# Block 3's two-direction recurrence: both directions in one set of tiles instead of one after the other

## The chip, the cores and the metric

The kernel runs on one core of a Trainium2 chip. Its engines work side by side, each through its own list of instructions: TensorE (PE; its weight loads are PEld), VectorE (DVE), ScalarE (ACT), GpSimd (POOL) and SyncE (SP), whose queue issues nearly all transfers from HBM. The metric is device time in microseconds (us). TensorE's clock has two levels here, 1.2 and 2.4 GHz, shown as a granted clock of 0.50 and 1.00.

## The reference

Three transformer blocks run one after the other on 256 tokens of width 1024, in fp32. The change is in the third block. Its input projection feeds a neighborhood attention, a memory attention, a recurrence (RWKV-7) in both directions, and three gates; the gated branches are merged, and an expert-choice layer with 16 experts of three weight matrices each follows. Of the recurrence (6 heads of 64 channels) this matters:

```python
for d in range(2):
    def mix(t, mu):
        return t + (token_shift(t, d) - t) * mu
    r = mix(p_r, mu_rkv[d, 0]); k = mix(p_k, mu_rkv[d, 1]); v = mix(p_v, mu_rkv[d, 2])
    w_log = -jax.nn.softplus(-(w0[d] + jnp.tanh(mix(lat_w, mu_w[d])) @ w2[d])) - 0.5
    decay = jnp.exp(-jnp.exp(w_log))
    a = jax.nn.sigmoid(a0[d] + mix(lat_a, mu_a[d]) @ a2[d])
    ...
    y_sum = y_sum + wkv7_scan(rh, to_heads_3(decay, RW_HEADS), kh, vh, -kk, kk * ah, reverse=(d == 1))
    bonus_sum = bonus_sum + jnp.sum(rh * kh * r_k, axis=-1, keepdims=True) * vh
```

`wkv7_scan` updates a 64 x 64 state per head with every token, from the first to the last for d = 0 and from the last to the first for d = 1. The two directions share no state; only their outputs are added, and a group norm over the sum follows.

## The kernel before

Matrix products with large weights are split: a weight tile w comes by DMA, ScalarE rounds it to wh (L303), VectorE takes the rest to wl (L305; four times GpSimd does it in this stage), and TensorE makes three products per tile, xh·wh, xl·wh and xh·wl (L314 to L316, output psg). Those of the third block's gates are called gate products here: 12 chunks of 48, 576 in all, and nothing in the recurrence needs them. A scheduler (Tile) writes each engine's list ahead of time and puts gate products between those of the recurrence and of the attentions.

`rwkv` runs the recurrence in a chunked form, two chunks of 128 tokens. For each direction in turn: the token shift is mixed in (subtractions on GpSimd L1353 and L1359, then VectorE L1354 and L1361); low-rank products plw and pla (L1369, L1370) and ScalarE's tanh give the decay and the gate a; VectorE sums the logarithm of the decay over a chunk with one scan per chunk and per 128 channels (L1387) and centres it (L1392); key norms (pnk), the bonus term (pbo), and the multiplication of keys and queries with the decays (L1438 to L1441) follow; v and bk are transposed on TensorE (pvt, pbt); the score products pka (L1465), masked, make 12 matrices of 128 x 128 (6 heads, 2 chunks), whose triangular inverse is needed.

`tri_inv` forms that inverse for n matrices at once. ScalarE copies the 32 x 32 blocks of the diagonal into one tile, VectorE transposes it (L550), eliminates in 14 steps of a multiplication and an addition (L560, L562), which work on all blocks at once in the other layout, and transposes back twice (L565, L566). TensorE then builds the larger blocks from the small ones (tpx, tpu: L575, L582, L604 to L633).

The scan itself goes chunk by chunk: masked scores pkm and pkr, then prh, psa and py, and pzt, which carries the state to the second chunk. `end` closes the recurrence with the group norm (pgm, pgv, pgg). The second direction begins with its own plw when the first one's last py are done, and its matrices are lower triangular, so tri_inv also has the mirrored form.

After it come the merges of the three branches (weights mg3a and mg3b, products psg on ona, omm and orw), the output product on mgh and mgl, the routing, and the experts. An expert's weights are loaded whole, 1 MB at a time, into slots: rings that exist all along, and the pools of which ES lists the sizes, which take over memory that earlier stages give up (`K.slots()` looks for it). SP issues its list in order; a load whose slot is still in use holds those behind it.

Of the kernel before, what the change touches and what calls it, by code (L numbers as in the profile page):

```python
# [25 lines left out]
def const_arrays():  # L26
# [4 lines left out]
    lo = (i > j).astype(np.float32)  # L31
# [12 lines left out]
    c["mk1"] = np.concatenate([lo, loi], 1)  # L44
# [40 lines left out]
    "b3": ["bd64", "mk1", "u16"],  # L85
    "b3a": ["mk0", "l16"],
# [135 lines left out]
ES = [2, 3, 1, 4, 3]  # L222
# [6 lines left out]
class Core:  # L229
# [308 lines left out]
    def tri_inv(self, first, pool, n, a, upper, want, out, tags):  # L538
        nc = self.nc
        P, W = [128, 1280], [128, max(1056, 96 * n)]  # L540
# [31 lines left out]
        px = self.psum([128, n, 32], "tpx")  # L572
        for i in range(n):
            for q in range(4):
                nc.tensor.matmul(px[qs[q], i], a[qs[q], i, qs[q]], mc[qs[q], i], start=True, stop=True)  # L575
        nc.vector.tensor_tensor(x, px, self.C("l16" if upper else "u16")[:, None, :].to_broadcast([128, n, 32]), op=ALU.mult)
        pu = []
        for lh, rh in ((oc, x), (x, oc)):
            pu.append(self.psum([128, n, 32], "tpu"))
            for i in range(n):  # L580
                for q in range(4):
                    nc.tensor.matmul(pu[-1][qs[q], i], lh[qs[q], i], rh[qs[q], i], start=True, stop=True)  # L582
        for d, p in zip((mc, oc), pu):
            nc.vector.tensor_tensor(d, d, p, op=ALU.add)
# [14 lines left out]
        px = self.psum([128, n, 32], "tpx")  # L599
        pm = self.psum([128, n, 32], "tpu")  # L600
        po = self.psum([128, n, 32], "tpu")
        for i in range(n):
            for r, c in pairs:
                nc.tensor.matmul(px[qs[r], i], a[qs[c], i, qs[r]], mc[qs[c], i], start=True, stop=True)  # L604
        for r, c in pairs:
            nc.scalar.copy(x[qs[r]], px[qs[r]])
        todo = [(r, c, half.start <= 32 * r < half.stop) for r, c in pairs]
        for i in range(n):
            for r, c, here in todo:
                if want == "m" or here:  # L610
                    nc.tensor.matmul(pm[qs[r], i], oc[qs[r], i], x[qs[r], i], start=True, stop=True)
        for i in range(n):
            for r, c, here in todo:
                if want == "o" or here:
                    nc.tensor.matmul(po[qs[c], i], x[qs[r], i], oc[qs[r], i], start=True, stop=True)
        for r, c in pairs:
            here = half.start <= 32 * r < half.stop
            (a0, p0, b0), (a1, p1, b1) = ((c, po, r), (r, pm, c)) if want == "o" else ((r, pm, c), (c, po, r))
            nc.vector.tensor_copy(out[qs[a0], :, qs[b0]], p0[qs[a0]])
            if here:  # L620
                nc.scalar.copy(oth[qs[a1], :, 32 * (b1 % 2):32 * (b1 % 2) + 32], p1[qs[a1]])
        x = w[:, 32 * n:96 * n].rearrange("p (i c) -> p i c", c=64)
# [696 lines left out]
def rwkv(K, keep, pool, tri, early, pp, lat, latg, y_out):  # L1319
# [18 lines left out]
    exps = []  # L1338

    for d in range(2):  # L1340
        sh = slice(0, S) if d == 0 else slice(2, S + 2)
        ar = pool.tile([128, 3, 2, S], F32, tag="ar", name="ar")
        bk = pool.tile([128, 3, 2, S], F32, tag="bk", name="bk")
        vs = pool.tile([128, 2, 3, S], F32, tag="vs", name="vs")
        vv, sq = vs[:, 0], vs[:, 1]
        aa = pool.tile(T3, F32, tag="aa", name="aa")
        km = pool.tile(T3, F32, tag="km", name="km")
        ce = pool.tile([128, 2, 3, 2, 129], F32, tag="om", name="ce")
        cn, ee = ce[:, 0], ce[:, 1]
        lm = early.tile([128, S], F32, tag="lm", name="lm")  # L1350


        nc.gpsimd.tensor_tensor(lm, lat[:, sh], lat[:, cur], op=ALU.subtract)  # L1353
        nc.vector.scalar_tensor_tensor(lm, lm, V("mu_wa", d), lat[:, cur], op0=ALU.mult, op1=ALU.add)  # L1354
        with K.behind(exps[0] if d else None):
            nc.scalar.activation(lm[0:64], lm[0:64], AF.Tanh)
        for n, dst in ((0, ar[:, :, 1]), (1, km), (2, vv)):
            src = pp[:, 3 * n:3 * n + 3]
            nc.gpsimd.tensor_tensor(dst, src[:, :, sh], src[:, :, cur], op=ALU.subtract)  # L1359
            for f in range(3):  # L1360
                nc.vector.scalar_tensor_tensor(dst[:, f], dst[:, f], V("mu_rkv", (d * 3 + n) * 3 + f), src[:, f, cur],  # L1361
                                               op0=ALU.mult, op1=ALU.add)


        for f in range(3):
            pw = K.psum([128, 2, 128], "plw")
            pa = K.psum([128, S], "pla")
            fs = slice(f * 128, f * 128 + 128)
            nc.tensor.matmul(pw, lora[0:64, d, fs], lm[0:64], start=True, stop=True)  # L1369
            nc.tensor.matmul(pa, lora[64:128, d, fs], lm[64:128], start=True, stop=True)  # L1370
            nc.scalar.activation(ee[:, f, :, 0:128], pw, AF.Tanh, scale=0.5,
                                 bias=hw0[:, 3 * d + f:3 * d + f + 1])
            tanh = nc.scalar.activation(aa[:, f], pa, AF.Tanh, scale=0.5, bias=ha0[:, 3 * d + f:3 * d + f + 1])
        hs = 0.5 * math.exp(-0.5)
        for f in range(3):
            e = ee[:, f, :, 0:128]
            nc.vector.tensor_scalar(e, e, hs, hs, op0=ALU.mult, op1=ALU.add)
        nc.vector.tensor_scalar(aa, aa, 0.5, 0.5, op0=ALU.mult, op1=ALU.add)

        o, z = (1, 0) if d == 0 else (0, 128)  # L1380
        for f in range(3):
            for c in range(2):
                src, dst = ee[:, f, c, 0:128], cn[:, f, c, o:o + 128]
                if d == 1:
                    src, dst = src[:, ::-1], dst[:, ::-1]
                nc.gpsimd.memset(cn[:, f, c, z:z + 1], 0.0)
                nc.vector.tensor_tensor_scan(dst, src, src, 0.0, op0=ALU.add, op1=ALU.bypass)  # L1387
        rho = pool.tile([128, 3, 2], F32, tag="rho", name="rho")
        nc.vector.tensor_copy(rho, cn[:, :, :, 64])
        for f in range(3):  # L1390
            for c in range(2):
                nc.vector.tensor_scalar(cn[:, f, c], cn[:, f, c], rho[:, f, c:c + 1], None, op0=ALU.subtract)  # L1392

        c0, c1 = (0, 1) if d == 0 else (1, 0)
        zc = pool.tile([128, 3], F32, tag="zc", name="zc")
        last = 128 if d == 0 else 0
        nc.vector.tensor_tensor(zc, cn[:, :, c0, last], rho[:, :, c1], op=ALU.add)
        nc.scalar.activation(zc, zc, AF.Exp, scale=-1.0)
        fl = lambda t: t.rearrange("p f c t -> p (f c t)")
        nc.scalar.activation(fl(ee), fl(cn), AF.Exp, scale=-1.0)  # L1400
        nc.scalar.activation(fl(cn), fl(cn), AF.Exp)


        kk = ar[:, :, 0]
        for f in range(3):
            nc.vector.tensor_scalar(kk[:, f], km[:, f], V("k_k", f), None, op0=ALU.mult)
        nc.scalar.activation(sq, kk, AF.Square)
        ln = K.ln_set(tanh)
        for f0, f1 in ((0, 2), (2, 3)):
            pn = K.psum([128, f1 - f0, S], "pnk")  # L1410
# [624 lines left out]
```

## Time and profile before

| | |
|---|---|
| median of 3 runs | 1989.26 us (1987.42 to 1989.70) |
| profiled execution | 1989.29 us, its span 1987.5 us |
| busy share of the span | PE 83%, PEld 54%, DVE 40%, ACT 30%, POOL 5% |
| mean granted TensorE clock | 0.918 |
| DMA | 557.20 MB, mean 280 GB/s |
| idle time of PE before expert products, mostly for DMA (L1887, L1959) | 154.6 and 49.4 us |

The first thing to read is the place of a stage on the time line: the first two blocks lie before about 750 us, the recurrence of the third from about 768 to 990, merges and routing to 1049, and the experts after it. The busy shares are means over these, with a different limit in each. A window's length less PE's busy time is PE's idle time in it.

### The profile page before, as it was taken

How to read it: one execution, taken by the hardware profiler on the slowest of the kernel's cores; microseconds unless marked ns; L12 is line 12 of the kernel's file. 1: busy time of each engine (PE TensorE's matmuls, PEld its weight loads, DVE VectorE, ACT ScalarE, POOL GpSimd, SP SyncE). 2: the span in 40 equal slices, each digit the busy share in tenths (PEclk: the TensorE clock that was granted, in tenths of full speed). 3: DMA queues.
4: the chain of work that ended last, by engine and by line, in shares of the span. 5: the costliest groups of instructions: out<-in, count | busy, mean ns of one | idle time of the engine just before them, and what ended most of it. 6: DMA issues, size and time to landing. Idle time of an engine off the chain costs nothing.

```text
span 1987.5 us, 28807 instructions
## 1 busy us (share of the span) xinstructions
PE 1657.6 (83%) x11882; PEld 1064.1 (54%) x11882; DVE 792.3 (40%) x1617; ACT 597.0 (30%) x1180; POOL 101.3 (5%) x140
## 2 busy tenths in 40 slices
PE   3999989999999999998989776777777677767776
PEld 2998989898999999777873111111111111111111
DVE  7798767657655577758472000000000000000001
ACT  3656455655555456534351000000000000000001
POOL 0000010000000110112011000000000000000000
PEclk9999989999999999979899988888878889877888
DMA  8443643345455554205388999999999999999998
GB/s 297 170 149 107 220 159 128 128 154 176 178 175 178 185 198 149 86 22 202 118 326 354 413 414 414 417 416 415 416 416 415 416 416 414 414 415 418 418 416 294
DMA packets 107062, 557.20 MB, mean 280 GB/s; under 512 B 10545, under 2 KB 17201, under 8 KB 62002
## 3 DMA queue, kind: packets, MB, share of 16 engines
q1 hardware_dynamic: 106930, 555.36, 71.9%
q8 instruction: 93, 1.52, 0.3%
q14 instruction: 39, 0.32, 0.0%
HBM read 554.27 MB, written 1.05 MB: 279 GB/s over the span
## 4 chain that ended last, share of the span: by engine, by line
PE 44%; DMA 43%; DVE 8%; ACT 2%; issue 1%; SPq 1%; POOL 0%; DVEq 0%; ACTq 0%; POOLq 0%
DMA w<-in_w_eu 12%; DMA w<-in_w_eg 11%; PE psg L316 10%; PE psg L314 10%; PE psg L315 10%; DMA w<-in_w_ed 7%; DMA wwh<-in_w_eu 4%; DMA wwl<-in_w_eg 4%; DMA wwh<-in_w_ed 3%; DVE wl L305 2%; PE pgu L1887 1%; DVE w L657 1%; PE pd L1959 1%; DMA wwh<-in_w_eg 1%; DMA wwl<-in_w_eu 1%
## 5 line engine op out<-in xcount | busy, mean ns | idle before, releaser
L1887 PE MATMUL pgu<-w,xe 128*32 128x512 f32 x1768 | 306.5, 788 | 154.6 <-DMA w<-in_w_eu 88.9
L305 DVE TENSOR_TENSOR wl<-w,wh 128x512 fp32r<-128x512 f32 (+1 forms) x510 | 330.1, 689 | 173.7 <-ACT wh L303 159.7
L303 ACT CAST wh<-w 128x512 fp32r<-128x512 f32 x516 | 288.1, 607 | 257.8 <-PE psg L315 223.8
L1887 PEld LDWEIGHTS pgu<-w,xe 128*32 128x32 f32 x1768 | 43.1, 122 | 396.6 <-DMA w<-in_w_eu 224.5
L1959 PE MATMUL pd<-w,at 128*32 128x512 f32 x808 | 183.7, 616 | 49.4 <-DMA w<-in_w_ed 44.1
L1937 DVE TENSOR_TENSOR gg<-gg,pgu 128x512 f32<-128x512 f32 x16 | 11.0, 688 | 508.0 <-PE pgu L1887 504.4
L1959 PEld LDWEIGHTS pd<-w,at 128*32 128x32 f32 x808 | 41.2, 112 | 183.0 <-DMA w<-in_w_ed 114.3
L1962 DVE COPY ye<-pd 128x512 f32<-128x512 f32 x15 | 10.4, 692 | 290.4 <-PE pd L1959 290.4
L1942 ACT COPY at<-pat 128x512 f32<-128x512 f32 x16 | 9.4, 585 | 311.5 <-PE pat L1940 311.5
L314 PE MATMUL psg<-h1h,wh 128*128 128x256 f32 x352 | 102.8, 292 | 0.0
L316 PE MATMUL psg<-h1h,wl 128*128 128x256 f32 x352 | 101.9, 290 | 0.0
L315 PE MATMUL psg<-h1l,wh 128*128 128x256 f32 x352 | 101.4, 288 | 0.0
L315 PE MATMUL psg<-n3hl,wh 128*128 128x256 f32 x344 | 100.7, 293 | 0.0
L316 PE MATMUL psg<-n3hh,wl 128*128 128x256 f32 x344 | 100.2, 291 | 0.4 <-DVE wl L305 0.4
L315 PE MATMUL psg<-n2fhl,wh 128*128 128x256 f32 x352 | 100.0, 284 | 0.2
L316 PE MATMUL psg<-n2fhh,wl 128*128 128x256 f32 x352 | 99.7, 283 | 0.0
L314 PE MATMUL psg<-n3hh,wh 128*128 128x256 f32 x344 | 99.6, 290 | 0.0
L314 PE MATMUL psg<-n2fhh,wh 128*128 128x256 f32 x352 | 99.5, 283 | 0.0
L1936 ACT ACTIVATE gg<-pgu 128x512 f32<-128x512 f32 x16 | 9.6, 597 | 277.5 <-PE pgu L1887 277.5
L314 PE MATMUL psg<-n2hh,wh 128*128 128x256 f32 x304 | 87.7, 289 | 2.0 <-ACT n2hh L456 2.0
L315 PE MATMUL psg<-n2hl,wh 128*128 128x256 f32 x304 | 88.4, 291 | 0.1
L316 PE MATMUL psg<-n2hh,wl 128*128 128x256 f32 x304 | 87.8, 289 | 0.0
(729 smaller groups left out, 3430.9 us busy)
## 6 DMA issues: line engine op xcount, KB each, us to landing
w<-in_w_eg SPq DMA_DIRECT2D x112, 1024.0 KB, 18.4
w<-in_w_eu SPq DMA_DIRECT2D x109, 1024.0 KB, 19.9
w<-in_w_ed SPq DMA_DIRECT2D x101, 1024.0 KB, 18.7
w<-in_w_in SPq DMA_DIRECT2D x68, 1024.0 KB, 4.9
w<-in_w_f SPq DMA_DIRECT2D x22, 1024.0 KB, 4.9
w<-in_w_ada SPq DMA_DIRECT2D x12, 1024.0 KB, 6.2
wwh<-in_w_ed SPq DMA_DIRECT2D x19, 512.0 KB, 14.8
wwl<-in_w_ed SPq DMA_DIRECT2D x19, 512.0 KB, 15.0
```

Source lines behind the costliest of these rows:

```text
L303: self.nc.scalar.copy(wh[:, a:b], w[:, k0 + a:k0 + b])
L305: e.tensor_tensor(wl[:, a:b], w[:, k0 + a:k0 + b], wh[:, a:b], op=ALU.subtract)
L314: nc.tensor.matmul(out, a, x[0], start=first, stop=False)
L315: nc.tensor.matmul(out, a, x[1], start=False, stop=False)
L316: nc.tensor.matmul(out, b, x[0], start=False, stop=last)
L657: nc.vector.scalar_tensor_tensor(w[:, f], w[:, f], 1.0, sg, op0=ALU.mult, op1=ALU.mult, accum_out=out[:, j:j + 1])
L1887: nc.tensor.matmul(pg[32 * j:32 * j + 32], xe[:, k, e * 32:e * 32 + 32], w[j // 2][:, j % 2 * 512:j % 2 * 512 + 512], start=k == 0, stop=k ...
L1936: nc.scalar.activation(gg, pgu[0], AF.Silu)
L1937: nc.vector.tensor_tensor(gg, gg, pgu[1], op=ALU.mult)
L1942: last = nc.scalar.copy(at, pt)
L1959: nc.tensor.matmul(pd[hh][32 * q:32 * q + 32], at[:, q, 32 * j:32 * j + 32], w[i][:, hh * 512:hh * 512 + 512], start=j == 0, stop=j == 3)
L1962: nc.vector.tensor_copy(ye[:, 512:1024], pd[1])
```

## The change

Both directions are worked on together. All tiles of the recurrence get a leading or middle index for the direction: 6 groups of 128 channels instead of 3, the second three in reversed time (the sources are read with a step of -1). Then both directions are causal in their own time, the matrices of both are upper triangular, and `tri_inv` is called once with 24 matrices. TensorE's work in it is cut in parts of 12 matrices. The logarithms of a direction's decay are summed by one scan of 774 elements, which a 0 in a tile `one` restarts at each of the six rows. One product of bk with the decay goes to GpSimd. v and bk are transposed behind the inverse instead of ahead of it. In the scan each kind of product is issued for both directions before the next kind. The tiles of the inverse and of the scan's outputs live in pools of their own on the right side of SBUF, those of the merges in a pool opened later, and ES goes from [2, 3, 1, 4, 3] to [3, 3, 5, 2], 13 as before. The number of TensorE's instructions doesn't change (9139); VectorE's falls from 1591 to 1503, ScalarE's from 1138 to 1117, GpSimd's from 145 to 128.

```diff
-ES = [2, 3, 1, 4, 3]
+ES = [3, 3, 5, 2]
...
+        parts = [(i, min(n, i + 12)) for i in range(0, n, 12)]
+        lev = self.C("l16" if upper else "u16")[:, None, :]
+        for i0, i1 in parts:
+            m = i1 - i0
+            px = self.psum([128, m, 32], "tpx")
...
-    for d in range(2):
-        sh = slice(0, S) if d == 0 else slice(2, S + 2)
-        ar = pool.tile([128, 3, 2, S], F32, tag="ar", name="ar")
-        bk = pool.tile([128, 3, 2, S], F32, tag="bk", name="bk")
+    ar = pool.tile([128, 6, 2, S], F32, tag="ar", name="ar")
+    bk = pool.tile([128, 6, 2, S], F32, tag="bk", name="bk")
...
+        for d in range(2):
+            t, c = src[:, :, sh[d]], src[:, :, cur]
+            if d:
+                t, c = t[:, :, ::-1], c[:, :, ::-1]
+            nc.gpsimd.tensor_tensor(dst[:, 3 * d:3 * d + 3], t, c, op=ALU.subtract)
...
-        for f in range(3):
-            for c in range(2):
-                src, dst = ee[:, f, c, 0:128], cn[:, f, c, o:o + 128]
...
-                nc.vector.tensor_tensor_scan(dst, src, src, 0.0, op0=ALU.add, op1=ALU.bypass)
+        nc.vector.tensor_tensor_scan(al(cn[:, ds]), one, al(ee[:, ds]), 0.0, op0=ALU.mult, op1=ALU.add)
...
-        nc.vector.tensor_tensor(ch(bk[:, :, 1]), ch(bk[:, :, 1]), cn[:, :, :, now], op=ALU.mult)
+    nc.gpsimd.tensor_tensor(ch(bk[:, :, 1]), ch(bk[:, :, 1]), cn[:, :, :, now], op=ALU.mult)
...
-        K.tri_inv(pool, tri, 12, ch12(am), d == 0, "o", ch12(om2), ("lr", "t2", "t3", "t4"))
+    with tc.tile_pool(name="tri", bufs=1, side="right") as tri:
+        K.tri_inv(tri, tri, 24, ch24(am), True, "o", ch24(om2), ("t1", "t2", "t3", "t4"))
...
+                ts, y = (cs, py) if d == 0 else (slice((1 - c) * 128, (2 - c) * 128), py[:, :, ::-1])
+                if c == 0:
+                    nc.scalar.copy(ysum[:, :, ts], y)
+                else:
+                    nc.vector.tensor_tensor(ysum[:, :, ts], ysum[:, :, ts], y, op=ALU.add)
...
+    lctx = ExitStack()
+    lp = lctx.enter_context(tc.tile_pool(name="l3", bufs=1))
+    orw = [lp.tile([128, 3, S], F32R, name=f"orw{i}") for i in range(2)]
+    gts[1] = lp.tile([128, 8, S], F32, name="g3b")
```

What this does to the engines' lists shows at three places; x48 stands for 48 instructions in a row (the trace records a product of fp32 operands, which all but psg have here, twice). The first is TensorE where the inverse passes from VectorE back to it, before in the second direction (tri tiles are the inverse's, psg gate products):

```order
L575 MATMUL tpx<-tri_9560,am 32x32 x48
L315 MATMUL psg<-n3hl,wh 128x256
L316 MATMUL psg<-n3hh,wl 128x256
L314 MATMUL psg<-n3hh,wh 128x256
L582 MATMUL tpu<-tri_9564,tri_9561 32x32 x48
L582 MATMUL tpu<-tri_9561,tri_9564 32x32 x48
L604 MATMUL tpx<-tri_9560,am 32x32 x24
```

Between its two halves stand seven gate products. Now, once for both directions (atps, atpt and atpo belong to the attentions):

```order
L576 MATMUL tpx<-tri_8976,am 32x32 x75
L481 MATMUL atps<-nak,naq 128x256 x2
L576 MATMUL tpx<-tri_8976,am 32x32 x21
L585 MATMUL tpu<-tri_8980,tri_8977 32x32 x48
L585 MATMUL tpu<-tri_8977,tri_8980 32x32 x13
L509 MATMUL atpt<-ct_g,atsm 128x128 x2
L585 MATMUL tpu<-tri_8977,tri_8980 32x32
L509 MATMUL atpt<-ct_g,atsm 128x128 x2
L585 MATMUL tpu<-tri_8977,tri_8980 32x32 x34
L585 MATMUL tpu<-tri_8980,tri_8977 32x32 x48
L585 MATMUL tpu<-tri_8977,tri_8980 32x32 x48
L608 MATMUL tpx<-tri_8976,am 32x32 x48
```

The number of tpx is the same over both, 96, and now in one place. Between the last pka and the first of these tpx there were 101 gate products and 32 products of the attentions in the first direction and 143 gate products in the second; now there are 133 and 27.

The second is TensorE in the scan's second chunk, before in the first direction:

```order
L1490 MATMUL pkr<-ar,bk 128x128 x6
L1500 MATMUL prh<-vt,lr 128x64 x3
L1505 MATMUL prh<-zt,ar 128x64 x3
L314 MATMUL psg<-n3hh,wh 128x256
L315 MATMUL psg<-n3hl,wh 128x256
L316 MATMUL psg<-n3hh,wl 128x256
L1500 MATMUL prh<-vt,lr 128x64 x3
L1505 MATMUL prh<-zt,ar 128x64 x3
L1510 MATMUL psa<-rh_9325,om_8919 128x64
L1515 MATMUL py<-lr,vt 64x128 x3
L1510 MATMUL psa<-rh_9325,om_8919 128x64 x5
L1519 MATMUL py<-ar,zt 64x128 x6
```

Four gate products stand between the first and the last prh here. Now:

```order
L1499 MATMUL pkm<-ar,bk 128x256 x12
L1506 MATMUL pkr<-ar,bk 128x128 x12
L1516 MATMUL prh<-vt,lr 128x64 x12
L1521 MATMUL prh<-zt,ar 128x64 x12
L312 MATMUL psg<-n3hl,wh 128x256
L313 MATMUL psg<-n3hh,wl 128x256
L311 MATMUL psg<-n3hh,wh 128x256
L1527 MATMUL psa<-rh_9714,om_8934 128x64 x2
L1527 MATMUL psa<-rh_9714,om_8934 128x64 x10
L1544 MATMUL py<-lr,vt 64x128 x6
L1549 MATMUL py<-ar,zt 64x128 x6
L1553 MATMUL py<-rt_9533,sa_9713 64x128 x6
```

Each kind stands for both directions in one row of products: 24 prh, 36 py. In both scans before there were 18 gate products or other psg, in the joint one 10. Before the last group-norm product pgg there are 171 fewer gate products than before it in the old program; 96 of them follow it in a row.

The third is SP's list from the last input weights (in_w_in) to the merge weights, before:

```order
L287 DMA w<-in_w_in 128x2048
L1870 DMA w<-in_w_eg 128x2048
L287 DMA w<-in_w_in 128x2048
L1870 DMA w<-in_w_eg 128x2048
L287 DMA w<-in_w_in 128x2048
L1870 DMA w<-in_w_eg 128x2048 x2
L287 DMA w<-in_w_mg3a 128x1280
L1870 DMA w<-in_w_eg 128x2048
L287 DMA w<-in_w_mg3a 128x1280 x3
L1870 DMA w<-in_w_eg 128x2048
L287 DMA w<-in_w_mg3b 128x768
```

Expert loads (w_eg) stand between input weights here. Now:

```order
L284 DMA w<-in_w_mg3a 128x1280
L1885 DMA w<-in_w_eg 128x2048 x6
L284 DMA w<-in_w_mg3a 128x1280
L1885 DMA w<-in_w_eg 128x2048 x2
L284 DMA w<-in_w_mg3a 128x1280
L1885 DMA w<-in_w_eu 128x2048
L284 DMA w<-in_w_mg3a 128x1280
L1885 DMA w<-in_w_eu 128x2048
L284 DMA w<-in_w_mg3b 128x768 x2
L1885 DMA w<-in_w_eu 128x2048
L284 DMA w<-in_w_mg3b 128x768 x2
```

All gate weights now go ahead of the expert loads, and six expert loads stand between the first and the second load of mg3a.

## Rows read from the trace of the kernel before

**Rows 1.** the page, slices of 49.7 us: GB/s moved by DMA.

```profile
GB/s 297 170 149 107 220 159 128 128 154 176 178 175 178 185 198 149 86 22 202 118 326 354 413 414 414 417 416 415 416 416 415 416 416 414 414 415 418 418 416 294
```

**Rows 2.** windows: stretch, length, busy us (instructions) of PE, PEld, DVE, ACT, POOL.

```profile
767.94:795.00 27.06, 25.63 (x192) 22.61 (x192) 26.31 (x59) 19.12 (x39) 2.22 (x2) 1.00 0.34 118
795.00:821.70 26.70, 24.30 (x152) 19.34 (x152) 21.42 (x58) 13.52 (x32) 3.89 (x5) 0.94 0.28 93
821.70:854.30 32.60, 31.51 (x576) 23.14 (x578) 20.57 (x53) 16.75 (x43) 6.31 (x7) 1.00 0.18 56
854.30:882.50 28.20, 26.97 (x195) 22.85 (x193) 9.44 (x20) 4.06 (x10) 3.62 (x9) 0.72 0.11 38
882.50:913.60 31.10, 28.76 (x199) 25.41 (x197) 28.67 (x58) 22.10 (x36) 10.84 (x9) 0.92 0.49 193
913.60:937.30 23.70, 17.42 (x148) 17.21 (x148) 21.05 (x42) 10.24 (x19) 3.06 (x4) 0.95 0.40 143
937.30:956.00 18.70, 17.22 (x495) 16.08 (x495) 7.58 (x11) 6.32 (x13) 1.00 (x2) 0.79 0.12 38
956.00:980.20 24.20, 23.47 (x203) 19.46 (x200) 7.93 (x18) 3.70 (x9) 0.00 (x0) 0.86 0.19 61
980.20:990.00 9.80, 9.80 (x66) 9.00 (x65) 7.42 (x15) 4.86 (x9) 0.00 (x0) 1.00 0.80 279
990.00:1012.00 22.00, 18.58 (x137) 16.80 (x135) 21.68 (x48) 14.47 (x27) 0.00 (x0) 1.00 0.70 254
1012.00:1049.40 37.40, 27.83 (x230) 26.29 (x230) 23.43 (x49) 16.49 (x30) 12.43 (x12) 0.89 0.89 349
```

**Rows 3.** timeline of PE: start, length, line, operation; the first expert product.

```profile
1049.44 1.08 PE L1887 MATMUL pgu<-w,xe 128*32 128x512 f32 x4
```

**Rows 4.** waits of PE, 767.94 to 990 us: total, times, longest.

```profile
PE tpx L575 <- DVE tri L565: 6.6, 2, 6.3
```

**Rows 5.** groups of DVE, second inverse: count, busy us, mean ns.

```profile
L305 DVE TENSOR_TENSOR wl<-w,wh 128x512 fp32r<-128x512 f32 x10 | 6.4, 686 | 0.8 <-ACT wh L303 0.8
L562 DVE TENSOR_TENSOR tri<-tri,tri 128x28 f32<-128x28 f32 (+6 forms) x14 | 5.2, 373 | 0.4
```

**Rows 6.** DVE on tile ce: ns minimum, median, maximum; first, last start.

```profile
L1387 DVE TENSOR_TENSOR_SCAN ce<-ce x12: 394/412/427, 770.3 to 889.6; 128x128 f32<-128x128 f32 x12
...
L1441 DVE TENSOR_TENSOR bk<-bk,ce x2: 950/1214/1477, 790.7 to 909.0; 128x768 f32<-128x768 f32 x2
```

**Rows 7.** DVE line L1406 in the second pass, the same columns.

```profile
L1406 DVE TENSOR_SCALAR ar<-km,vt x3: 340/1556/1659, 881.2 to 884.3; 128x256 f32<-128x256 f32 x3
```

**Rows 8.** timeline of POOL at the same moment.

```profile
881.24 1.47 POOL L1359 TENSOR_TENSOR ar<-pp 128x768 f32<-128x768 f32 x1 [0.88 <-PE py L1519]
882.72 1.47 POOL L1359 TENSOR_TENSOR vs<-pp 128x768 f32<-128x768 f32 x1
```

**Rows 9.** windows at the lower clock; PE clock stands behind POOL.

```profile
866.80:883.90 17.10, 17.10 (x93) 14.62 (x90) 5.32 (x7) 2.42 (x6) 3.54 (x9) 0.50 0.18 62
887.30:890.70 3.40, 3.40 (x11) 2.87 (x11) 3.40 (x12) 1.81 (x3) 0.00 (x0) 0.50 0.00 0
935.10:941.90 6.80, 4.63 (x208) 4.34 (x212) 4.78 (x4) 0.40 (x1) 0.00 (x0) 0.50 0.03 6
945.30:948.70 3.40, 3.40 (x16) 3.40 (x17) 0.54 (x1) 3.16 (x7) 0.00 (x0) 0.50 0.02 5
972.60:979.40 6.80, 6.80 (x41) 5.57 (x40) 0.43 (x1) 1.92 (x5) 0.00 (x0) 0.50 0.20 58
```

**Rows 10.** timeline of PE, first scan, second chunk.

```profile
867.83 1.54 PE L1500 MATMUL prh<-vt,lr 128*128 128x64 f32 x6
```

**Rows 11.** timeline of PE, second scan.

```profile
959.82 0.88 PE L1500 MATMUL prh<-vt,lr 128*128 128x64 f32 x6
...
965.53 1.59 PE L1483 MATMUL pkm<-ar,bk 64*128 64x256 f32 x10
...
969.38 0.88 PE L1500 MATMUL prh<-vt,lr 128*128 128x64 f32 x6
```

More of the change, by code (lines that the diff above doesn't have):

```diff
@@ L608, in tri_inv @@
-        for i in range(n):
-            for r, c, here in todo:
[L610 to L621, printed above, removed]
@@ L622, in tri_inv @@
-        x = w[:, 32 * n:96 * n].rearrange("p (i c) -> p i c", c=64)
+        todo = [(r, c, half.start <= 32 * r < half.stop) for r, c in pairs]
+        for i0, i1 in parts:
+            m = i1 - i0
+            px = self.psum([128, m, 32], "tpx")
+            for i in range(i0, i1):
+                for r, c in pairs:
+                    nc.tensor.matmul(px[qs[r], i - i0], a[qs[c], i, qs[r]], mc[qs[c], i], start=True, stop=True)
+            for r, c in pairs:
+                nc.scalar.copy(x[qs[r], i0:i1], px[qs[r]])
@@ new lines, in rwkv @@
+    nc.vector.tensor_scalar(aa, aa, 0.5, 0.5, op0=ALU.mult, op1=ALU.add)
+    zc = pool.tile([128, 6], F32, tag="zc", name="zc")
+    nc.vector.tensor_tensor(zc, cn[:, :, 0, 128], rho[:, :, 1], op=ALU.add)
+    nc.scalar.activation(zc, zc, AF.Exp, scale=-1.0)
+    nc.scalar.activation(al(ee), al(cn), AF.Exp, scale=-1.0)
+    nc.scalar.activation(al(cn), al(cn), AF.Exp)
+    kk = ar[:, :, 0]
+    for f in range(3):
+        nc.vector.tensor_scalar(two(kk, f), two(km, f), V("k_k", f), None, op0=ALU.mult)
@@ new lines, in rwkv @@
+    nc.scalar.activation(sq, kk, AF.Square)
+    ln = K.ln_set(tanh)
+    for j0 in (0, 2, 4):
+        pn = K.psum([128, 2, S], "pnk")
+        for j in range(2):
+            nc.tensor.matmul(pn[:, j], C("bd64"), sq[:, j0 + j], start=True, stop=True)
+        nc.vector.tensor_scalar(sq[:, j0:j0 + 2], pn, 1e-24, None, op0=ALU.max)
+    with K.behind(ln):
+        nc.scalar.activation(sq, sq, AF.Ln, scale=2.0 ** 20)
+    exp = nc.scalar.activation(sq, sq, AF.Exp, scale=-0.5, bias=K.sc(SC_10LN2))
@@ new lines, in rwkv @@
+    nc.vector.tensor_tensor(kk, kk, sq, op=ALU.mult)
+    nc.vector.tensor_tensor(bk[:, :, 0], kk, aa, op=ALU.mult)
+    for f in range(3):
+        nc.vector.tensor_scalar(two(aa, f), two(aa, f), V("k_a", f), oka[:, f:f + 1], op0=ALU.mult, op1=ALU.add)
+    nc.vector.tensor_tensor(bk[:, :, 1], km, aa, op=ALU.mult)
+    for f in range(3):
+        nc.vector.scalar_tensor_tensor(two(sq, f), two(ar[:, :, 1], f), V("r_k", f), two(bk[:, :, 1], f),
+                                       op0=ALU.mult, op1=ALU.mult)
@@ new lines, in rwkv @@
+    for j0 in (0, 2, 4):
+        pb = K.psum([128, 2, S], "pbo")
+        for j in range(2):
+            nc.tensor.matmul(pb[:, j], C("bd64"), sq[:, j0 + j], start=True, stop=True)
+        nc.vector.tensor_tensor(sq[:, j0:j0 + 2], pb, vv[:, j0:j0 + 2], op=ALU.mult)
+    nc.gpsimd.tensor_tensor(bonus, sq[:, 0:3], sq[:, 3:6, ::-1], op=ALU.add)
+    ch = lambda t: t.rearrange("p f (c t) -> p f c t", c=2)
+    prev, now = slice(0, 128), slice(1, 129)
+    nc.vector.tensor_tensor(ch(ar[:, :, 0]), ch(ar[:, :, 0]), ee[:, :, :, prev], op=ALU.mult)
@@ L1460, in rwkv @@
+    nc.vector.tensor_tensor(ch(bk[:, :, 0]), ch(bk[:, :, 0]), cn[:, :, :, now], op=ALU.mult)
+    nc.gpsimd.tensor_tensor(ch(bk[:, :, 1]), ch(bk[:, :, 1]), cn[:, :, :, now], op=ALU.mult)
+    nc.vector.tensor_tensor(ch(ar[:, :, 1]), ch(ar[:, :, 1]), ee[:, :, :, now], op=ALU.mult)
+    ectx.close()
+    am = pool.tile([128, 2, 2, 6, 128], F32, tag="sk", name="am")
+    mk = C("mk0").rearrange("p (a t) -> p a t", a=2)
+    for d in range(2):
         for c in range(2):
@@ new lines, in rwkv @@
+    bt = pool.tile([128, 2, 2, 384], F32, tag="vv", name="bt")
+    for n in range(2):
+        for d in range(2):
+            pt = K.psum([128, 384], "pbt")
+            for f in range(3):
+                nc.tensor.transpose(pt[:, f * 128:f * 128 + 128], bk[:, 3 * d + f, n, 0:128], ident)
+            nc.scalar.copy(bt[:, n, d], pt)
+    with tc.tile_pool(name="post", bufs=1, side="right") as post:
+        rt2 = post.tile([128, 2, 2, 6, 128], F32, name="rt2")
+        zt = post.tile([128, 6, 64], F32, name="zt")
+        dh = [(d, h) for d in range(2) for h in range(6)]
+        for c in range(2):
+            cs = slice(c * 128, c * 128 + 128)
+            lr = pool.tile([128, 2, 6, 2, 128], F32, tag="sk", name="lr")
+            for f in range(3):
+                pks = [K.psum([128, 2, 2, 128], "pkm") for _ in range(2)]
+                for d in range(2):
@@ L1496, in rwkv @@
-            prs = [K.psum([128, 3, 64], "prh") for _ in range(2)]
-            for f in range(3):
-                for hh, pr in enumerate(prs):
-                    h = 2 * f + hh
-                    nc.tensor.matmul(pr[:, f], lr[:, h, 0], vt[:, c, h * 64:h * 64 + 64], start=f == 0,
-                                     stop=ci == 0 and f == 2, skip_group_check=True)
-            if ci == 1:
-                for f in range(3):
+                    nc.vector.tensor_tensor(lr[:, :, 2 * f + hh], pk, mk[:, None].to_broadcast([128, 2, 2, 128]), op=ALU.mult)
@@ new lines, in rwkv @@
+            for d in range(2):
+                pks = [K.psum([128, 3, 128], "pkr") for _ in range(2)]
+                for f in range(3):
+                    for pk, s64 in zip(pks, halves):
+                        nc.tensor.matmul(pk[:, f], bk[s64, 3 * d + f, 0, cs], ar[s64, 3 * d + f, 1, cs], start=True, stop=True)
+                for hh, pk in enumerate(pks):
+                    nc.vector.tensor_tensor(rt2[:, c, d, hh::2], pk, mk[:, 1:2].to_broadcast([128, 3, 128]), op=ALU.mult)
+            sa = post.tile([128, 2, 6, 64], F32, tag="sa3", name="sa3")
@@ new lines, in rwkv @@
+            rh = post.tile([128, 2, 6, 64], F32, tag="rh3", name="rh3")
+            prs = [K.psum([128, 6, 64], "prh") for _ in range(2)]
+            for j in range(6):
+                for hh, pr in enumerate(prs):
+                    d, h = j // 3, 2 * (j % 3) + hh
+                    nc.tensor.matmul(pr[:, j], lr[:, d, h, 0], vt[:, c, d, h * 64:h * 64 + 64], start=j == 0,
+                                     stop=c == 0 and j == 5, skip_group_check=True)
+            if c == 1:
+                for j in range(6):
@@ L1566, in end @@
         return i
-    return exps[1], end
+    return exp, end
 class TwoNorms:
@@ L1635, in block3 @@
     W = A["w_in3"]
-    orw = [npool.tile([128, 3, S], F32R, name=f"orw{i}") for i in range(2)]
     ona = [npool.tile([128, 3, S], F32R, name=f"ona{i}") for i in range(2)]
```

313 lines of the change are left out of this document (124 added, 189 removed).

## The prediction

> **What bounds the kernel now.** I read the page first. Its slices show DMA at 413 to 418 GB/s from about 1090 us to the end [rows 1]: the expert stage, more than 900 us long, is bound by its weight loads. Its first product starts at 1049.44 us [rows 3]. By the order view 21 expert loads precede the first wait for an expert slot, and they do in the changed program too. So the stage keeps its length as long as those loads are in place, and the time moves one for one with the moment at which TensorE reaches 1049.44.
>
> Next I read the windows up to there [rows 2]. The stretch from 767.94 (the first low-rank product of the recurrence) to 1049.44 is eleven pieces. TensorE is the busiest engine in most of them, and the number of its products is the same in both programs. What can move the start of the experts is therefore only idle time of TensorE and its clock, whichever piece the gate products stand in. Idle is length less busy time, in order: first pass 1.43 (low-rank products to the score products pka), 2.40 (inverse on VectorE), 1.09 (inverse on TensorE), 1.23 (scan); second pass 2.34, 6.28, 1.48, 0.73; then 0.00, 3.42 (merges) and 9.57 (routing, which the change doesn't touch). The first eight make 16.98. The waits name the largest: 6.3 us until VectorE's last transposes in the second inverse [rows 4]. The windows at the lower clock (0.50, 1.2 GHz) are the other cost: 17.10 and 6.80 us in the scans, 3.40, 6.80 and 3.40 in the second pass outside its scan [rows 9].
>
> **The change part by part.** The sum is made against the profiled execution, 1989.3 us (span 1987.5 and 1.8 around it), which is the median of the runs shown.
>
> 1. *One inverse instead of two.* VectorE does the elimination once: 28 multiplications and additions at about 0.37 us, 10.4 us, and three transposes are gone. They were not all on the path: TensorE worked on gate products meanwhile. What counts is the wait for the result, 2.40 + 6.28 = 8.68 before. How long is the one that stays? In the first pass 101 gate products and 32 of attention stood between pka and the inverse's first product tpx, in the second 143 gate products alone; now there are 133 and 27. A gate product takes about 0.12 us (17.42 us busy for 148 instructions, 143 of them gates [rows 2]), so the cover is nearer the first pass's. Against it, ScalarE copies twice as much into the block, and VectorE splits about three more weights than in the first pass at 0.69 [rows 5]. I take 3.5: **−5.2**. Bounds 2.4 and 6.3: −6.3 to −2.4.
>
> 2. *Low-rank products to pka.* VectorE was busy 26.31 + 28.67 of 58.16 us, TensorE 25.63 + 28.76 [rows 2]: both nearly full. The joint pass takes from VectorE twelve scans at 0.41 [rows 6] for two of 774 elements, which no row shows (the cost of the 128-element one as a floor, six of them, 2.5, as a ceiling); the centring in single rows; one product of bk with the decay, 0.95 to 1.48 us a pass [rows 6], which goes to GpSimd; and the second direction's mixing, which now lies ahead of 767.94. TensorE loses the transposes of v and bk to a later place, and 17 gate products. Both get shorter by similar amounts, so I leave the idle time at 3.8: **0**. Lower bound −2 (half of it goes). Upper bound +7.4: the 28 us by which the stage outgrows one pass run with the idle share of the second inverse (6.28 of 23.70).
>
> 3. *TensorE's part of the inverse and attention:* 1.09 + 1.48 before. The products come in two parts of 12 matrices, so one part runs while the other is evacuated: **0**, ±1.5.
>
> 4. *Scan.* 1.23 + 0.73 before, mostly at the masked scores. The order shows both directions' products in one line, each wait once per chunk, but for a block twice the size: **+0.5** (−1 to +2).
>
> 5. *GpSimd beside VectorE.* Three VectorE scalings of 256 elements in line L1406 took 340, 1556 and 1659 ns [rows 7], while GpSimd ran a subtraction of 768 elements for 1.47 us [rows 8]; 340 is what one costs undisturbed at most. So a GpSimd operation held VectorE by about 1.2 us. The changed kernel has six such subtractions next to the mixing, and the bk product of 1536 elements, by the same row some 2.9 us, right between VectorE's decay products. The Trainium skill's GPSIMD Engine Reference (Key points) says that GpSimd shares its SBUF interfaces with VectorE and contends with two-input instructions; the trace agrees, 1556 beside 340 ns. I take **+2** for those that fall on the path; nothing if hidden by gate products, +4 if the product of 2.9 us and one subtraction both hold the chain.
>
> 6. *Merges.* 171 gate products leave the part before the last group-norm product; 96 of them follow it in a row. The 3.42 us of idle [rows 2] arose where merge products waited for gates and split weights, so part of it should fill: **−1.9** (−3.4 to 0). What was shifted behind isn't lost: the number of products is the same.
>
> 7. *Lower clock outside the scans.* The second pass's own stretches held 3.40 + 4.63 + 3.40 = 11.4 us of busy time at half the clock [rows 9]; at the full one they'd need 5.7 less. That at 935.10 follows the 6.28 us wait. The joint pass will have some of its own: half of it saved, **−3** (−5.7 to 0).
>
> 8. *Clock in the scan.* From the second chunk's first prh product, the first scan took 14.67 us (867.83 to 882.50), all at 0.50 but for its end; the second 10.82 (969.38 to 980.20) [rows 10, 11]. In the joint scan prh products come 24 in a row, py 36 (by the order's count; the trace records each twice), with 10 gate products in all where the two scans had 18. If both directions go like the first scan it is +3.9 (2 × 14.67 − 25.49), if like the second −3.9. Longer rows of small products look more like the first: **+2**. The far ends are in the rivals.
>
> Sum: −5.2 + 0 + 0 + 0.5 + 2 − 1.9 − 3 + 2 = −5.6, so 1983.7 us.
>
> **The rivals.**
>
> *The joint scan drops to half clock in its first chunk* (slower). Place: after the first chunk's prh, 12 in a row by the order where it was six. For it: at 867.83 six prh took 1.54 us, at 959.82 0.88, ×1.75, and the stretch from 866.80 was busy throughout (17.10 of 17.10 us [rows 9]), so a busy TensorE did lose its clock among small products. Against: in neither scan did it fall in the first chunk. Price: 959.82 to 965.53 is 5.71 us a direction [rows 11]; twice that at 0.75 more is +8.6, and the second chunk at +3.9 instead of +2. Sum 1994.2. It decides from the point where the first chunk's py products show 0.50.
>
> *A busy TensorE keeps its clock* (much faster). The joint scan has no long idle gap. Then the 23.90 us at 0.50 in the scans [rows 9] shrink to 57% (0.88 over 1.54), −10.3 instead of +2: 1971.4. Against it stands the same 17.10 of 17.10. The Trainium skill's TensorE: Matmul & The Clock Gate (HAM oscillation) names idle gaps as what takes the clock down; by that rule this case would be the likely one, and the stretch from 866.80 speaks against it.
>
> *The gain goes back in the low-rank stage* (no measurable change). One chain of double-sized VectorE and ScalarE work leaves TensorE without split weights or inputs: the upper bound of 2, +7.4, gives 1991.1; half of it gives 1987.4. For it: VectorE was busy 97% of the first pass's stage.
>
> *Expert loads in front of merge weights* (slower). The order now has six expert loads between the first and the second mg3a load on SP. They need the slots of the recurrence's pools. At 414 GB/s [rows 1] one of 1.05 MB takes 2.5 us, six 15.2, and the merge weight follows 1.6 later. If slots come free at the scan's end, 9.80 us before the last group-norm product [rows 2], it lands 7 us after that product; 96 gate products cover 11.5. So it decides from slots that come free 4.5 us after the scan's end on. At ten after it the wait is 5.5 and the sum 1989.2; if the third and fourth mg3a load, behind two more expert loads and one, come late by as much as they are long (2 × 2.5 and 2.5) besides, 1997 to 1999.
>
> Otherwise the prefetch is no limit: from 980.20 to 1049.40 the DMA engines were idle 2.0 + 6.6 + 4.1 us, and the recurrence ends some 20 us (171 × 0.12) earlier against the experts' start, which holds the eight gate-expert loads (20 us) that lose their early places.
>
> **How the numbers follow.** Forecast 0.33 and kept clock 0.08 make faster by over 0.2% (4 us, what a measurement of this kernel can tell from no change) 0.41. The low-rank stage is 0.27, no change. Half clock 0.22, loads 0.07, GpSimd's contention beyond its bound 0.03: slower 0.32. The range goes from the kept clock (1971) to the worst of the loads (1999), which takes in the bounds of 1 to 8; the forecast's own is 1979 to 1986.
>
> **What would show it.** One wait of tpx for the transposes, of 2.4 to 6.3 us. TensorE's idle time from the first low-rank product to the last group-norm product of 12 to 14 us, before 16.98. That last product near 962 to 970. PE clock 0.50 in the second chunk alone. No wait of merge products for DMA. The prediction is wrong if the idle time is above 20 us, if the first chunk's py run at 0.50, or if the first expert product starts after 1049.

## The result: 1977.91 us, and the profile after

The changed kernel takes 1977.91 us (median, 1976.87 to 1979.57) beside 1989.48 for the one before: a ratio of 0.9943 (95% interval 0.9926 to 0.9961), 11.6 us faster. On a second chip the ratio was 0.9956 (0.9942 to 0.9970). The forecast was 1983.7 within 1971 to 1999, and 1979 to 1986 for the sum itself. The direction holds, but the gain is twice the forecast one and lies 1 us outside the sum's own range (on the second chip, at 1980.48, inside it), and its parts are not those of the sum.

The first expert product of the changed kernel, in the timeline of TensorE (start, length, line, operation):

```profile
1039.65 2.57 PE L1902 MATMUL pgu<-w,xe 128*32 128x512 f32 x16
```

It was at 1049.44 [rows 3]: 9.8 us earlier, and the span is 9.9 shorter (1977.6). So the step that ties the time to the start of the experts is right; in the ten profiles of this case 938 to 940 us lie between the first expert product and the end. The stages of the changed kernel (windows, columns as in [rows 2]; 740 to the first low-rank product at 778.5, to the last pka, inverse on VectorE to the first tpx, inverse on TensorE with attention and transposes, scan, to the last pgg, merges, routing):

```profile
740.00:778.50 38.50, 34.99 (x262) 34.05 (x260) 23.29 (x35) 16.44 (x31) 8.56 (x6) 0.91 0.43 152
778.50:830.70 52.20, 47.84 (x347) 43.20 (x346) 43.04 (x57) 31.16 (x55) 17.03 (x10) 0.97 0.31 108
830.70:856.30 25.60, 24.48 (x172) 20.73 (x171) 21.41 (x61) 15.87 (x32) 2.14 (x3) 1.00 0.30 112
856.30:915.50 59.20, 51.10 (x1065) 41.63 (x1064) 27.05 (x66) 25.66 (x60) 6.86 (x6) 0.77 0.17 51
915.50:952.90 37.40, 35.91 (x396) 31.76 (x395) 14.23 (x24) 6.90 (x15) 0.00 (x0) 1.00 0.20 83
952.90:962.50 9.60, 9.60 (x62) 8.79 (x63) 2.96 (x5) 4.82 (x8) 0.00 (x0) 1.00 0.82 328
962.50:1002.00 39.50, 37.57 (x303) 36.47 (x303) 33.67 (x69) 23.61 (x45) 3.00 (x2) 1.00 0.84 306
1002.00:1039.60 37.60, 28.34 (x235) 26.60 (x233) 23.32 (x49) 16.21 (x29) 13.45 (x12) 0.88 0.82 310
```

Length less PE busy time (the idle time) is 3.51, 4.36, 1.12, 8.10, 1.49, 0.00, 1.93 and 9.26 us. The first low-rank product comes at 778.5, it came at 767.94. The inverse's wait fell from 8.68 us to 1.12, but 5.5 us more idle time stand in TensorE's part of the inverse and 3.5 ahead of the low-rank products. From 740 to the start of the experts TensorE idles as long as before: 29.77 now; [rows 2] add up to 29.97, and in the 28 us ahead of them it had not waited. The idle time didn't change, it moved; what fell is TensorE's busy time. (Up to the 5605th product, at 730.0 us before and 733.4 now, this execution was 3.4 us behind, with the same idle time and a clock of 0.98 for 0.99, in blocks that the change leaves alone; so the stage gained 13.)

The busy time fell in the scan, which takes 37.40 us at clock 1.00 for both directions. [rows 2] have 28.20 and 24.20, 15.0 more, of which only 0.5 is idle time and about 1 is gate products (10 instead of 18). The products of the second chunk, in the timeline of TensorE:

```profile
940.20 2.89 PE L1516 MATMUL prh<-vt,lr 128*128 128x64 f32 x24
...
945.87 2.34 PE L1527 MATMUL psa<-rh,om 128*128 128x64 f32 x20
...
949.74 0.88 PE L1553 MATMUL py<-rt,sa 128*64 128x128 f32 x12
```

24 prh take 2.89 us, 0.72 for six. Six took 1.54 in the first scan and 0.88 in the second [rows 10, 11]. The clock stayed up, and the rows are denser even where the clock was up before.

The lower clock has not left the kernel. Its stretches after (windows, clock behind POOL):

```profile
754.30:761.10 6.80, 6.09 (x29) 6.07 (x29) 2.52 (x3) 1.14 (x2) 0.67 (x1) 0.50 0.45 154
815.70:819.10 3.40, 3.40 (x15) 3.22 (x15) 3.40 (x5) 0.00 (x0) 1.04 (x1) 0.51 0.86 308
860.10:870.30 10.20, 7.30 (x333) 5.74 (x335) 5.17 (x15) 1.91 (x8) 1.27 (x1) 0.50 0.45 151
873.80:884.00 10.20, 9.14 (x155) 7.38 (x143) 0.56 (x1) 3.12 (x5) 0.45 (x1) 0.50 0.02 3
890.80:897.60 6.80, 6.80 (x95) 6.62 (x93) 5.38 (x14) 3.78 (x11) 1.84 (x2) 0.50 0.29 73
```

PE was busy in them for 32.7 us, in those of [rows 9] for 35.3. Three of the five now lie in TensorE's part of the inverse, where its 32 x 32 products lose less by the clock than the scan's products do (last section). TensorE's timeline shows waits of 1.3 to 2.4 us that end less than 3 us ahead of four of them; ahead of the one at 890.80 it shows none.

### The profile page after: what moved, and what is told of

Its sections match the earlier page's. It is cut to its first block, busy times and chain, and to the rows that moved or that the text cites. A ratio compares the mean times of both kernels' runs of the same rounds, so it can differ in the third digit from the quotient of the medians.

```text
span 1977.6 us, 28659 instructions
## 1 busy us (share of the span) xinstructions
PE 1649.7 (83%) x11882; PEld 1062.5 (54%) x11882; DVE 771.7 (39%) x1529; ACT 590.2 (30%) x1159; POOL 106.8 (5%) x123
## 4 chain that ended last, share of the span: by engine, by line
PE 46%; DMA 41%; DVE 8%; ACT 2%; issue 1%; SPq 1%; POOL 1%; DVEq 0%; ACTq 0%
DMA w<-in_w_eg 15%; DMA w<-in_w_eu 13%; PE psg L313 10%; PE psg L311 10%; PE psg L312 10%; DMA w<-in_w_ed 5%; DMA wwl<-in_w_eu 4%; DVE wl L302 2%; PE pgu L1902 2%; PE pd L1974 2%; DMA wwh<-in_w_eu 1%; DVE w L664 1%; DMA wwl<-in_w_eg 1%; DMA wwh<-in_w_eg 1%; PE psg L328 1%
## 5 line engine op out<-in xcount | busy, mean ns | idle before, releaser
L1976 ACT COPY ye<-pd 128x512 f32<-128x512 f32 x15 | 8.8, 585 | 264.6 <-issue 257.3
```

## The experiments

Means of the runs of one kernel stand beside the medians here, since single runs of one kernel differ by 4 to 21 us on the two chips of the experiments; the kernel before has medians of 1989.47 and 1989.25 there.

**The scan alone undone.** Joint preparation and the one inverse stay; TensorE's list is the same up to the first masked score.

```diff
-        for c in range(2):
-            lr = pool.tile([128, 2, 6, 2, 128], F32, tag="sk", name="lr")
+        for d in range(2):
+            for c in range(2):
+                lr = pool.tile([128, 6, 2, 128], F32, tag="sk", name="lr")
...
+                pa = K.psum([128, 6, 64], "psa")
+                for h in range(6):
+                    nc.tensor.matmul(pa[:, h], om2[:, d, c, h], rh[:, h], start=True, stop=True)
```

> The changed kernel with one thing undone: the scan runs direction by direction again (both chunks of the first, then both chunks of the second); the joint preparation and the one inverse stay, and TensorE's list is the same up to the first masked score. Theory A (the gain lies in the scan: rows of like products of both directions keep the full clock and switch less): the scan grows from 37 us to 45 to 50, part of it at clock 0.50, and the time goes to 1985 to 1990. Theory B (the gain lies in the inverse that is done once, and the scan's clock was chance): the scan stays under 41 us and the time within 1977 to 1981.

Measured: 1985.23 us (mean 1985.5 of 10 runs), ratio 0.9985 (0.9970 to 1.0000). The scan took 46.7 us, 9.3 more than the joint one, with 6.8 of them at the lower clock, here in the windows from its first masked score to its end and of that stretch:

```profile
916.30:963.00 46.70, 45.29 (x413) 37.44 (x413) 15.02 (x30) 7.39 (x19) 0.00 (x0) 0.93 0.19 68
933.60:940.40 6.80, 6.80 (x41) 5.58 (x41) 0.00 (x0) 0.68 (x2) 0.00 (x0) 0.50 0.00 1
```

The same products at either level in this one scan, in the timeline of TensorE:

```profile
934.92 2.40 PE L1526 MATMUL psa<-rh,om 128*128 128x64 f32 x10
937.25 1.54 PE L1542 MATMUL py<-lr,vt 128*64 128x128 f32 x10
...
958.66 1.33 PE L1526 MATMUL psa<-rh,om 128*128 128x64 f32 x10
...
960.72 0.87 PE L1547 MATMUL py<-ar,zt 64*64 64x128 f32 x12
```

Ten psa took 2.40 and 1.33 us, py products 1.54 and 0.87 in rows of ten and twelve. Of the 9.3 us, about 2 are gate products that the scheduler put into this stretch (28 instead of 10), so that they are missing from another. Theory A holds for the scan: it is worth 6 to 8 us on top of the rest (1979.1 is the mean of the nearest thing to the changed kernel on this chip, v mixed later, below), and the clock is part of it. Two windows of the same run say more, the time from TensorE's last wait to the fall at 933.60, and the second direction:

```profile
928.40:933.60 5.20, 5.20 (x42) 4.34 (x43) 2.17 (x5) 0.35 (x2) 0.00 (x0) 1.00 0.00 0
941.10:962.30 21.20, 20.50 (x203) 16.81 (x201) 6.86 (x14) 3.23 (x8) 0.00 (x0) 1.00 0.01 2
```

The clock fell behind 5.2 us without a wait. And the second direction, with the same rows of products as the first, kept the full clock, so a scan by direction doesn't always lose it. Twice its 21.2 us is 42.4, 5.0 more than the joint scan at the same clock. About 1 of these is eight more gate products; the other 4 are what the denser rows of the joint scan are worth without the clock (an estimate).

**The inverse alone undone.**

```diff
-        K.tri_inv(tri, tri, 24, ch24(am), True, "o", ch24(om2), ("t1", "t2", "t3", "t4"))
+        for d in range(2):
+            K.tri_inv(tri, tri, 12, ch12(am[:, d]), True, "o", ch12(om2[:, d]), ("t1", "t2", "t3", "t4"))
```

> The changed kernel with the inverse called twice, 12 matrices each, one after the other; both upper triangular, the joint preparation and the joint scan stay. Theory A (scan): the scan's products still cost 34 to 36 us and the time stays within 1976 to 1983, the second elimination lying beside gate products. Theory B (inverse): the 8 us of waits for the inverse come back, 1985 to 1988.

Measured: 1986.15 us (mean 1985.9 of 10, from 1979.7 to 1992.0), ratio 0.9985 (0.9963 to 1.0006). The scan's products kept the full clock, as theory A wants; the time came out as theory B wants. Neither alone is right. The profiled execution, 1981.9 and so among the quick ones of its kernel, shows the waits for the inverse again:

```profile
PE tpx L576 <- DVE tri L562: 4.4, 1, 4.4
...
PE tpu L585 <- DVE tri L577: 1.9, 1, 1.9
...
PE tpu L585 <- issue: 1.4, 1, 1.4
```

**Both undone.** The two edits above together.

> The changed kernel with both undone: the inverse is called twice and the scan runs direction by direction; the joint preparation stays. The two single undoings cost 7.6 and 8.0 us by the means of their runs (1985.5 and 1985.9 beside 1977.9), more together than the whole gain of 11.5. If they add up: 1992 to 1995, slower than the kernel before, so that the joint preparation by itself costs 3 to 5. If the two share one cause (what one stage leaves idle the other gets back): 1986 to 1989.

Measured: 1994.42 us (mean 1993.9 of 10), ratio 1.0020 (1.0003 to 1.0038): slower than the kernel before. Beside this kernel the one inverse brings 8.4 (to 1985.5), the joint scan 8.0 (to 1985.9), and both 14 to 15 (to 1979.1 and 1980.3, the means nearest to and of the changed kernel on these chips). So the gains nearly add up, and what is left of the change costs 4.6 (1993.9 beside 1989.3; 1 to 8 by the interval). That is the joint preparation, but also the later transposes, the product on GpSimd and the new pools; this run doesn't separate them. The scan's clock fell again, twice for 6.80 us:

```profile
946.60:953.40 6.80, 6.80 (x42) 5.58 (x44) 0.00 (x0) 0.52 (x2) 0.00 (x0) 0.50 0.00 0
970.50:977.30 6.80, 6.80 (x42) 5.58 (x44) 0.00 (x0) 0.97 (x2) 0.00 (x0) 0.50 0.00 0
```

TensorE was busy all of that time. No gate product stood between these scans' products, so gate products among them are not needed for a fall. Right ahead of either fall it had waited 0.26 us for ScalarE's copy of rh:

```profile
946.46 0.59 PE L1528 MATMUL psa<-rh,om 128*128 128x64 f32 x2 [0.26 <-ACT rh L1525]
```

With the scan alone undone no wait stood ahead of the fall (above), but three gate products stood at it. So neither is needed by itself. The joint scan has both, waits of up to 0.35 us and 10 gate products, and kept its clock.

**Where the preparation costs: the square of the keys.** In the changed kernel's timeline of ScalarE the square waits 5.70 us at the head of the list for VectorE's mixing, and four roundings of weights (wh) stand behind it:

```profile
743.55 0.58 ACT L1696 COPY pp<-psg 128x512 f32<-128x512 f32 x1
749.82 1.48 ACT L1418 ACTIVATE sk<-ar 128x1536 f32<-128x1536 f32 x1 [5.70 <-DVE ar L1417]
751.21 2.16 ACT L300 CAST wh<-w 128x512 fp32r<-128x512 f32 x4
```

```diff
-    nc.scalar.activation(sq, kk, AF.Square)
+    with K.behind(tanh):
+        nc.scalar.activation(sq, kk, AF.Square)
```

> The changed kernel with ScalarE's square of the keys held behind the tanh of the low-rank products. In the changed kernel that square stands at the head of ScalarE's list from 744.1 to 749.8, waits for VectorE's mixing, and the roundings of input weights queue behind it; TensorE then waits 3.3 us and loses its clock for 6.8. If that is what the joint preparation costs: 1972 to 1975. If the mixing on VectorE holds the weights anyway, or the key norms now come late: 1977 to 1980.

Measured: 1975.03 us (mean 1973.4 of 5), ratio 0.9924 (0.9897 to 0.9950); the changed kernel beside it on the same chip gave 1980.48 (mean 1980.3 of 10, 0.9956). Windows of 730 to 770 us, first of that run of the changed kernel, then with the edit:

```profile
730.00:770.00 40.00, 36.99 (x288) 35.88 (x288) 26.51 (x41) 17.77 (x33) 10.12 (x6) 0.96 0.44 158
```

```profile
730.00:770.00 40.00, 38.89 (x320) 38.28 (x319) 29.08 (x44) 18.30 (x36) 10.42 (x6) 1.00 0.50 175
```

Idle time 3.0 against 1.1 us, clock 0.96 against 1.00. All five runs with the edit are faster than all ten of the changed kernel. That is the square's hold, shown; by the medians it gives back 5.5, about what the rest of the change cost.

> The changed kernel itself beside the others on the same chip. 1976 to 1980 if the figures of different chips can be compared; the scan's products at 34 us and the full clock again.

Measured: 1980.48 us, just above what was expected; the scan again took 37.4 us, with TensorE busy for 35.9, at clock 1.00.

**Two more edits.** Mixing v later, by moving its lines behind the key norms:

> The changed kernel with the token shift of v moved behind the key norms; TensorE's list is unchanged. In the changed kernel TensorE waits 3.3 us for split weights between 744 and 755 and then runs 6.8 us at clock 0.50, while VectorE and GpSimd mix. If the mixing ahead of the low-rank products causes that: 1972 to 1976. If the mixing only moves to a stage where VectorE is as full: 1977 to 1980.

Measured: 1979.53 us (mean 1979.1 of 8), ratio 0.9942. This tells nothing of the mixing: the scheduler put v's mixing back to the same place, 748.56 on VectorE against 749.71. An edit in the source isn't always one in the list.

The product with the decay on VectorE (`nc.gpsimd` to `nc.vector` in that line):

> The changed kernel with the product of bk and the decay back on VectorE; on GpSimd it took 4.63 us, and the masked scores waited 1.7 us behind GpSimd's bonus. If GpSimd's share is a cost on the path (term 5 of the prediction, +2): 1975 to 1977.5. If it is hidden and VectorE is the tighter engine there: its 1.75 us come onto the path, 1979 to 1980.

Measured: 1979.76 us (mean 1979.2 of 9, from 1969.2 to 1988.7), ratio 0.9955 (0.9931 to 0.9980): no difference that can be told from the changed kernel. GpSimd had taken 4.63 us for it, in its timeline:

```profile
818.06 4.63 POOL L1450 TENSOR_TENSOR bk<-bk,ce 128x1536 f32<-128x1536 f32 x1 [6.19 <-DVE sk L1436]
822.65 3.34 POOL L1443 TENSOR_TENSOR bonus<-sk 128x768 f32<-128x768 f32 x1
```

With the square's edit too:

> The square held behind the tanh, and the product of bk and the decay on VectorE. If the square's hold is the cost: 1971 to 1976, and the fewer waits of products for instructions that the profile with the decay on VectorE showed (3.0 us instead of 6.4) come on top. If neither matters: 1977 to 1980.

Measured: 1972.72 us (mean 1974.4 of 6), ratio 0.9925 (0.9902 to 0.9947). It beats the kernel before and the changed one, and isn't told apart from the square's edit alone. What the expectation calls waits for instructions are waits whose cause the profile doesn't show ("issue").

## Why the prediction was right, and where not

1. *The inverse* (−5.2): the wait fell by 7.6, beyond the bound of −6.3. By runs the one inverse is worth 7 to 8 us, and with it called twice the waits come back (4.4 and 1.9 us). The cover by gate and attention products fits that; it was taken too cautiously.
2. *Low-rank products to pka* (0): +0.6 in idle time. Right. What the step missed lies ahead of 767.94: it moved the second direction's mixing there and gave that place no price. There stand 3.5 us of idle time and 6.8 at the lower clock, most of them through the square in ScalarE's list: with its edit the idle time of 730 to 770 fell from 3.0 to 1.1 us.
3. *TensorE's part of the inverse* (0, ±1.5): +5.5, the worst miss among the idle terms. The waits, largest groups:

```profile
PE tpu L585 <- issue: 5.3, 2, 2.9
PE pbo L1441 <- DVE sk L1436: 1.8, 1, 1.8
PE atps L481 <- DVE atsm L494: 1.7, 1, 1.7
PE pka L1463 <- DVE am L1465: 1.4, 1, 1.4
PE pkm L1499 <- DVE lr L1501: 1.1, 4, 0.4
PE tpx L608 <- issue: 1.1, 1, 1.1
```

 5.3 + 1.1 us of "issue" are waits for nothing that the profile shows. These waits go with the one inverse: at tpu and tpx they make 2.6 to 7.4 us in the profiles that have it, 1.4 and 1.5 in the two variants with the inverse called twice, and 1.5 in the kernel before. The step had no such wait in it.
4. *Scan, idle* (+0.5): −0.5, within its bounds, though of the other sign.
5. *GpSimd* (+2): not told from 0 for the product with the decay. The operation was longer (4.63 for 2.9), and taking it off GpSimd gave nothing measurable. If an engine was held there, it was GpSimd: VectorE's product of the same size beside it (L1449, at 817.90) took 1.75 us, and 1.75 with the decay on VectorE too. VectorE was held in the mixing, which the edit left as it was. Three of its scalings, with GpSimd's subtractions beside the middle one:

```profile
743.63 0.47 DVE L1417 TENSOR_SCALAR ar<-sk,vt 128x512 f32<-128x512 f32 x1
...
745.23 1.69 DVE L1417 TENSOR_SCALAR ar<-sk,vt 128x512 f32<-128x512 f32 x1
...
749.31 0.48 DVE L1417 TENSOR_SCALAR ar<-sk,vt 128x512 f32<-128x512 f32 x1
```

```profile
744.20 4.04 POOL L1376 TENSOR_TENSOR vv<-pp 128x768 f32<-128x768 f32 x2 [2.76 <-ACT pp L1696]
```

 The 1.2 us lie inside the 5.70 for which the square waits.
6. *Merges* (−1.9): −1.5. Right. No merge product waited for DMA (the waits there are for split weights and gates), so the rival of loads ahead of merge weights fell.
7. *Lower clock outside the scans* (−3): wrong. Busy time at the lower clock outside the scans rose from 11.4 us (the three stretches of the second pass) to 32.7. The cost was smaller than these figures. From 740 us to the experts TensorE was busy outside the scan for 229.0 us before and 233.9 now, of which 3.3 are the 28 products by which this execution was behind; so the same products took some 1.6 us more (1 of them the gate products that left the scan), where the step had −3. That the inverse's 32 x 32 products lose less by the clock was not foreseen, and the lower clock's own share wasn't measured by itself.
8. *Clock in the scan* (+2): wrong in sign, and the largest miss. The step took longer rows of small products for those that lose the clock. Its evidence was the stretch from 866.80, busy throughout; it didn't look at what stood ahead of it, a wait of 1.23 us:

```profile
865.43 0.70 PE L1483 MATMUL pkm<-ar,bk 64*128 64x256 f32 x2 [1.23 <-DVE lr L1485]
```

 The second scan's fall at 972.60 came without one, 5 us after the last wait. (The first scan also stood at 0.50 up to its end, not "but for its end".) In all profiles with the joint scan (the changed kernel twice, and five of its variants) the scan stood at 1.00; in all three kernels with a scan by direction part of it stood at 0.50, five of six directions, each in its second chunk. The rival of a kept clock, given 0.08, came true for this part, and was priced at 10.3. Of the 15.0 us by which the scan got shorter, about 10 are the clock (52.4 against twice the 21.2 of a direction that kept it), 1 is gate products and 4 are denser rows (0.72 for six prh where it was 0.88 at the same clock). The sum had no term for the rows.

The range held since the misses partly cancel, which is luck: the runs give −6 to −8 for the scan where the sum had +2.5, and −8 for the inverse with +5 for the preparation and what comes with it where it had −5.2 and, for the clock and GpSimd, −1. Of the signs that the prediction named, the last group-norm product (962.5) and the start of the experts came as said. The wait for the inverse (1.12 us), the idle time up to the last group-norm product (15.07 for 12 to 14) and the lower clock in the second chunk did not.

Of the clock rule in the Trainium skill (TensorE: Matmul & The Clock Gate, HAM oscillation) the runs show a limit: with the scan alone undone the clock fell to 0.50 behind 5.2 us without a wait and stayed there for 6.80 us in which TensorE was busy throughout, so the absence of gaps isn't enough. Why rows of both directions keep the clock is not settled. What is shown is that they did in seven profiles, that a scan by direction mostly did not, and that neither gate products nor waits are, by themselves, needed for a fall.

## What to carry to other kernels

Two chains that ran one after the other gained twice here when they went side by side: fewer serial waits, and denser rows on the engine that both use. What they need first also comes together, so look at the heads of the in-order lists at that place: one operation that waits there holds up work that has nothing to do with it. Undo the parts one at a time and then all at once; here each undoing alone cost more than half of the gain, and only the joint one showed that a third part had taken some back.

## What the runs showed of the hardware

- Several long rows of 32 x 32 products are followed by a gap in TensorE's work that has no releaser. The changed kernel's timeline of TensorE:

```profile
861.63 1.46 PE L585 MATMUL tpu<-tri,tri 32*32 32x32 f32 x92
865.98 0.64 PE L585 MATMUL tpu<-tri,tri 32*32 32x32 f32 x27 [2.90 <-issue]
...
868.02 3.05 PE L585 MATMUL tpu<-tri,tri 32*32 32x32 f32 x223
873.43 0.53 PE L585 MATMUL tpu<-tri,tri 32*32 32x32 f32 x35 [2.37 <-issue]
```

 After 92 (with 45 just ahead of them), 2.90 us; after 223, 2.37; in the kernel before 1.48 after 150 in the second inverse, and none in the first, where attention products break the rows. With the decay on VectorE such a gap follows 177:

```profile
879.29 1.71 PE L585 MATMUL tpu<-tri,tri 32*32 32x32 f32 x177
883.37 0.27 PE L585 MATMUL tpu<-tri,tri 32*32 32x32 f32 x3 [2.37 <-issue]
```

 The profile doesn't show the cause.

- Those products lose less at the lower clock than others. The 92 above lie wholly in the stretch at 0.50 from 860.10 to 870.30 and took 1.46 us, 15.9 ns each. In the first inverse of the kernel before, at clock 1.00 [rows 2], 84 took 0.92, 11.0 ns each:

```profile
824.52 0.92 PE L582 MATMUL tpu<-tri,tri 32*32 32x32 f32 x84 [0.64 <-DVE tri L576]
```

 The ratio is 1.4, where it is 1.8 for psa (2.40 to 1.33). So a stretch at the lower clock costs less where such products fill it than in the scan.
